# Two pairs of feed-forward input units by seven block products in place of eight, weight block sums on VectorE and by DMA

## The chip, the cores and the metric

The kernel runs on one core of a Trainium2 chip. The number that counts is the device time of one execution in microseconds (us). Three executions of the kernel before took 1249.81, 1249.92 and 1251.14 us; the median is 1249.92 us.

## What is computed

A decoder trunk of two layers on 256 tokens of width 1024, everything in float32. Each layer is a feed-forward half step, a mixer of three attention branches, and a second feed-forward half step, each followed by a residual sum and a layer norm. There are thus four feed-forward steps and two mixers. The change touches the feed-forward steps alone in what is computed:

```
D_MODEL = 1024;  SEQ = 256;  DEPTH = 2;  D_FF = 2816

def swiglu(x, w_in, w_out):
    gate, up = jnp.split(x @ w_in, 2, axis=-1)
    return (jax.nn.silu(gate) * up) @ w_out

for l in range(DEPTH):
    x = layer_norm(DN_ALPHA * x + 0.5 * swiglu(x, ffn1_in[l], ffn1_out[l]), ln_g[l, 0], ln_b[l, 0])
    x = layer_norm(DN_ALPHA * x + hybrid_mixer(x, ...), ln_g[l, 1], ln_b[l, 1])
    x = layer_norm(DN_ALPHA * x + 0.5 * swiglu(x, ffn2_in[l], ffn2_out[l]), ln_g[l, 2], ln_b[l, 2])
```

## The kernel before

**Tiles.** The tokens are two tiles of 128 (t = 0 and 1). The activations stand transposed in SBUF, eight blocks of 128 rows (the k of the code) by 128 tokens. Every float32 operand is split in two parts in the matmul's input format: a high part (`XH`, made by a copy on ScalarE) and a low part, the rest (`XL`, made by a subtraction on VectorE). One block product is three matmuls of 512 columns into a PSUM bank: high by high, high by low, low by high (lines 474, 475, 476, in `products`).

**Weights.** They come from HBM in chunks of 128 x 1024 float32, two blocks of k by 512 columns, on the SP queue (`weights`, line 230) into one of five buffers `raw`. ScalarE writes a chunk's high part (line 240) and VectorE its low part (line 249) into a pair of the 30 buffers `r`. A chunk is used by both token tiles, 2 x 2 x 3 = 12 matmuls, and its pair is then free again.

**A feed-forward step.** The 2816 hidden columns are 11 units of 256 columns. An input unit (`in_unit`) reads 256 gate and 256 up columns, side by side in one bank, over eight k: 4 chunks, and 8 x 3 = 24 matmuls for a token tile, 48 for both. Then `h_chain` makes silu(gate) times up (line 517 on ScalarE, line 519 on VectorE), transposes it on TensorE (line 371) and splits it (lines 383 and 385). An output unit (`out_unit`) multiplies it with its 256 rows of `w_out`: 2 chunks, 24 matmuls. The order is input unit u, then output unit u - 2.

**What sets the order.** The program is written once, in Python, by a planner. `items` is the list of chunk uses in order; the main loop at the end of the kernel steps a virtual clock `vt`, lets tile 1 follow tile 0 by up to `LAG` = 7 items, and between two block products issues whatever is due on the other engines, with estimated costs for VectorE (`V`), ScalarE (`A`) and the DMA. What it writes is fixed: on the chip each engine goes through its own list in that order and waits on semaphores.

**Layer norm.** `layer_norm` (lines 429 to 452) adds the output to the residual, takes mean and variance, subtracts and scales both halves of a tile's row (line 447, two instructions), then applies the reciprocal deviation and the bias to both halves (line 452, two instructions). After each half of line 452, `x_parts` transposes it for the next step. GpSimd computes the deviation's power (line 440) and issues the loads of gain and bias (`load_gb`, line 418).

## Time and profile before

| | before |
|---|---|
| median of three executions | 1249.92 us |
| the profiled execution | 1251.66 us, of which the trace's span is 1249.9 us |
| TensorE (PE) busy | 1236.2 us, 99% of the span |
| VectorE (DVE) busy | 883.8 us, 71% |
| ScalarE (ACT) busy | 640.9 us, 51% |
| DMA queues | 215.60 MB on the SP queue, 6.29 MB on GpSimd's |
| granted TensorE clock | 1.00 in every slice but the first (0.95) |

The span holds the six stages one after the other. By the matmuls' tiles the first feed-forward step runs to about 186 us, the first mixer to 431, the next two feed-forward steps to 623 and 811, the second mixer to 1048, the last feed-forward step to 1241; the rest is the last layer norm and the store. A busy TensorE in this profile is not a TensorE at its peak, since matmuls overlap: the distance from one matmul's start to the next one's tells what it costs.

### The profile page before, as it was taken

The page shows a single profiled execution, that of the slowest core. Times are in us where ns is not written, and L with a number is a line of the kernel's source. Part 1 is how long each engine was busy: PE and PEld are TensorE (multiplying, and loading weights), DVE is VectorE, ACT ScalarE, POOL GpSimd, SP SyncE. Part 2 cuts the span into 40 slices and gives each one's busy share as a digit, 9 for nine tenths or more (in the row PEclk, how much of TensorE's full clock was granted, in tenths as well). Part 3 has the DMA queues.
Part 4 walks back from the last instruction along what each step waited for, and adds up shares of the span by engine and source line. Part 5 has one row for each costly group of instructions (what it writes and reads, how often), then busy time and mean ns, then how long its engine had stood idle before and what let it go on. Part 6 is the DMA issues. An engine that isn't in the chain of part 4 may idle for free. (4 is left out here: it accounts for less than half of the span.)

```text
span 1249.9 us, 16651 instructions
## 1 busy us (share of the span) xinstructions
PE 1236.2 (99%) x5897; PEld 1025.5 (82%) x5897; DVE 883.8 (71%) x1533; ACT 640.9 (51%) x1005; POOL 32.5 (3%) x78
## 2 busy tenths in 40 slices
PE   8999999999999999999999999999999999999997
PEld 6888888888888888888888888888888887888886
DVE  6656559996999975555675555699979999655454
ACT  7544445566676554444444444454666756444340
POOL 0100000000000000000000000000000000000000
PEclk9999999999999999999999999999999999999999
DMA  9866656454535766655556655655444377656630
GB/s 313 267 183 197 203 150 183 132 150 144 179 102 178 237 207 203 204 181 176 172 186 227 203 182 179 170 152 156 146 136 153 101 222 237 216 170 200 185 118 34
DMA packets 173235, 222.95 MB, mean 178 GB/s; under 512 B 19040, under 2 KB 113248, under 8 KB 173152
## 3 DMA queue, kind: packets, MB, share of 16 engines
q1 hardware_dynamic: 171168, 215.60, 55.8%
q0 software_dynamic: 1984, 6.29, 1.6%
q8 instruction: 46, 0.75, 0.2%
q14 instruction: 37, 0.30, 0.1%
HBM read 220.80 MB, written 1.05 MB: 177 GB/s over the span
## 5 line engine op out<-in xcount | busy, mean ns | idle before, releaser
L249 DVE TENSOR_TENSOR r<-raw,r 128x1024 fp32r<-128x1024 f32 (+1 forms) x408 | 491.2, 1219 | 130.2 <-ACT r L240 77.8
L240 ACT ACTIVATE r<-raw 128x1024 fp32r<-128x1024 f32 (+1 forms) x408 | 420.0, 1052 | 125.5 <-PE bank L475 40.6
L474 PE MATMUL bank<-r,xh 128*128 128x512 f32 (+1 forms) x1184 | 468.9, 396 | 0.3 <-ACT xh L383 0.3
L476 PE MATMUL bank<-r,xl 128*128 128x512 f32 (+1 forms) x1184 | 461.9, 390 | 0.7 <-DVE xl L385 0.6
L475 PE MATMUL bank<-r,xh 128*128 128x512 f32 (+1 forms) x1184 | 461.3, 390 | 0.5 <-DVE r L249 0.5
L476 PEld LDWEIGHTS bank<-r,xl 128*128 128x128 f32 x1184 | 222.5, 188 | 48.4 <-DVE xl L385 2.0
L475 PEld LDWEIGHTS bank<-r,xh 128*128 128x128 f32 x1184 | 223.0, 188 | 43.1 <-DVE r L249 1.2
L474 PEld LDWEIGHTS bank<-r,xh 128*128 128x128 f32 x1184 | 222.8, 188 | 42.1 <-ACT xh L383 0.5
L474 PE MATMUL bank<-r,r 128*128 128x512 f32 x448 | 181.7, 406 | 0.0
L476 PE MATMUL bank<-r,r 128*128 128x512 f32 x448 | 175.7, 392 | 0.4 <-DVE r L385 0.4
L475 PE MATMUL bank<-r,r 128*128 128x512 f32 x448 | 175.1, 391 | 0.0
L517 ACT ACTIVATE f<-bank 128x256 f32<-128x256 f32 x88 | 33.8, 384 | 191.3 <-PE bank L476 190.4
L383 ACT ACTIVATE r<-bank 128x256 fp32r<-128x256 f32 (+1 forms) x120 | 52.2, 442 | 136.4 <-PE bank L371 136.2
L385 DVE TENSOR_TENSOR r<-bank,r 128x256 fp32r<-128x256 f32 (+1 forms) x120 | 58.3, 491 | 71.5 <-ACT r L383 71.3
L519 DVE TENSOR_TENSOR f<-f,bank 128x256 f32<-128x256 f32 x88 | 36.7, 417 | 96.0 <-ACT f L517 95.6
L476 PEld LDWEIGHTS bank<-r,r 128*128 128x128 f32 x448 | 84.1, 188 | 19.3 <-DVE r L385 1.2
L475 PEld LDWEIGHTS bank<-r,r 128*128 128x128 f32 x448 | 84.5, 189 | 14.7
L474 PEld LDWEIGHTS bank<-r,r 128*128 128x128 f32 x448 | 84.2, 188 | 14.2
L371 PE MATMUL bank<-ident,f 128*128 128x128 f32 x464 | 75.9, 273 | 0.6 <-DVE f L867 0.6
L371 PEld LDWEIGHTS bank<-ident,f 128*128 128x128 f32 x464 | 59.2, 141 | 20.5 <-DVE f L867 1.1
L791 ACT ACTIVATE f<-f,nb 128x128 f32<-128x128 f32 (+1 forms) x96 | 42.4, 445 | 9.0 <-DVE nb L783 8.7
L383 ACT ACTIVATE xh<-bank 128x512 fp32r<-128x512 f32 x32 | 18.6, 594 | 36.0 <-PE bank L371 36.0
(110 smaller groups left out, 691.8 us busy)
## 6 DMA issues: line engine op xcount, KB each, us to landing
raw<-in_ffn_in_dram SPq DMA_DIRECT2D x352, 256.0 KB, 3.7
raw<-in_w_in_dram SPq DMA_DIRECT2D x96, 512.0 KB, 3.6
raw<-in_ffn_out_dram SPq DMA_DIRECT2D x88, 512.0 KB, 4.9
raw<-in_w_out_dram SPq DMA_DIRECT2D x16, 512.0 KB, 4.7
raw<-in_w_br_a_dram SPq DMA_DIRECT2D x8, 512.0 KB, 4.2
raw<-in_w_br_c_dram SPq DMA_DIRECT2D x8, 512.0 KB, 4.1
raw<-in_w_br_b_dram SPq DMA_DIRECT2D x8, 512.0 KB, 3.7
f<-in_ln_g_dram POOLq DMA_DIRECT2D x12, 256.0 KB, 4.2
```

The costliest lines, as they stand in the source:

```text
L240: act.activation(pair[0].t[:, :n], raw_t[c % RAWS][:, :n], AF.Copy)
L249: dve.tensor_tensor(lo, raw_t[c % RAWS][:, :n], h.bitcast(F32), op=OP.subtract)
L371: pe.transpose(bank[:, j * 128:(j + 1) * 128], src[:, j * 128:(j + 1) * 128], ident)
L383: act.activation(hi, v, AF.Copy)
L385: dve.tensor_tensor(lo, v, hi.bitcast(F32), op=OP.subtract)
L474: pe.matmul(o, lhsT=xh(k), rhs=wh, start=k == 0, stop=False)
L475: pe.matmul(o, lhsT=xh(k), rhs=wl, start=False, stop=False)
L476: pe.matmul(o, lhsT=xl(k), rhs=wh, start=False, stop=k == nk - 1)
L517: act.activation(s.t[:, :256], ps.t[:, :256], AF.Silu)
L519: dve.tensor_tensor(s.t[:, 256:], s.t[:, :256], ps.t[:, 256:], op=OP.mult)
L791: act.activation(p.t[:, i * n:(i + 1) * n], p.t[:, i * n:(i + 1) * n], AF.Exp, bias=nb[:, h:h + 1], scale=SCALE, accum_out=den[:, h:h + 1])
```

## The change

The four input units 4, 5, 7 and 8 of a feed-forward step become two pairs, D4 (units 4 and 5) and D7 (7 and 8). A pair's work is a 2 x 2 block product: rows are the two token tiles, the inner dimension is the lower and the upper half of k (four k each), columns are 512 gate and 512 up columns. Eight block products of 12 matmuls are replaced by Strassen's seven (in Winograd's form), P1 to P7 (`double`). Each serves one chunk use, not two.

- The sums of activation blocks (`s_chain`): once in a feed-forward step, 10 additions or subtractions of 128 x 512 on VectorE and four splits, each a copy on ScalarE and a subtraction on VectorE.
- The sums of weight blocks: for a pair, two chunks of upper-half up weights are loaded into two double buffers `wide`; VectorE adds them to the gate chunks (line 328, 128 x 1024), later adds two more pairs of chunks. For P7 the lower-half up weights, already loaded once, are read again from HBM by a DMA on GpSimd's queue that adds to what stands in `wide` (line 318).
- The seven products need 14 prepared chunks (high and low part), where the two units needed 8.
- Results are put together in three PSUM banks: ScalarE copies a bank (line 707) before the next product accumulates onto it, VectorE adds or subtracts (lines 718 and 720). `c11`, `c21` and `h_pair` then make silu(gate) times up for 512 columns at once.
- The buffers: `raw` 5 to 7, `r` 30 to 28, small buffers `f` 16 to 12 and the two `wide` buffers, whose four halves also serve as `f`.
- Order: the string `FFN` gives the sequence of units. Near the pairs tile 1 follows by 2 items (`NEAR`). `layer_norm` now scales the second half (`centre(1)`) after the first half's line 452 work; the gain and bias load moves from unit 9 to unit 10.

```diff
-RAWS = 5
-NR = 30
+RAWS = 7
+NR = 28
+DEEP = 9
+EARLY = 2
 KEEP = 2
-NF = 16
+NF = 12
+FFN = "0 1 o0 2 o1 3 o2 D4 o3 6 o4 o5 D7 o6 9 o7 10 o8 o9 o10"
+NEAR = 2
...
+    wide_t = [tile_of(f"wide{i}", [128, 1024]) for i in range(2)]
+    f_t += [w[:, h * 512:(h + 1) * 512] for w in wide_t for h in range(2)]
...
     def weights(hold):
+        if sum_next[0] < len(sums):
+            n, pieces, c, chain, behind = sums[sum_next[0]]
+            ats = [low_at.get(b) for b in behind] if behind else [landed.get(chain)]
+            if None not in ats and max(ats) <= vt[0] + 1.0:
+                for view, ap in pieces:
+                    nc.gpsimd.dma_start(out=view(chain.view(n)), in_=ap, accum_op=OP.add)
+                clk["dma"] = max(clk["dma"], max(ats) + 0.5, vt[0] + 1.0) + 3.0
+                arrive[c] = clk["dma"] + 1.5
+                sum_next[0] += 1
+        if add_next[0] < len(adds):
+            c, other, there, behind, gone = adds[add_next[0]]
+            if (all(low_at.get(b, 1e9) <= vt[0] + AHEAD for b in behind)
+                    and max(arrive.get(there, 0.0), landed.get(there, 0.0)) <= vt[0] + AHEAD
+                    and (there in arrive or there in landed) and clk["dve"] <= vt[0] + AHEAD):
+                f = chunks[c].chain.view(1024)
+                dve.tensor_tensor(f, f, other(), op=OP.add)
+                low_at["sum", c] = V(1024)
+                arrive[c] = low_at["sum", c] + SEM
+                add_next[0] += 1
+                if gone is not None:
+                    give(gone, low_at["sum", c])
+        c = prep[high_next[0]] if high_next[0] < len(prep) else None
+        if (c in arrive and arrive[c] <= vt[0] + AHEAD and c - pos[0] < DEEP
                 and clk["act"] <= vt[0] + (1.0 if c - pos[0] < 3 else AHEAD)
-                and (pair := R.take_many(2, 0 if c - pos[0] < 3 else KEEP))):
-            n = chunks[c][0]
+                and (pair := R.take_many(2, 0 if c - pos[0] < 3 else KEEP + held[0]))):
...
+        def centre(h):
+            dve.scalar_tensor_tensor(y[:, hv[h]], y[:, hv[h]], mv[:, 0:1], (g0, g1)[h].t, op0=OP.subtract, op1=OP.mult)
             V(512)
+        centre(0)
+        if last:
+            centre(1)
         yield clk["dve"]
         for h, b in enumerate((b0, b1)):
-            hs = slice(h * 512, (h + 1) * 512)
+            hs = hv[h]
+            if h and not last:
+                centre(1)
...
+        def s_chain():
+            def tt(out, a, b, op):
+                dve.tensor_tensor(out, a, b, op=op)
+                return V(512) + 0.05
...
+            yield tt(a.t, h21, h22, OP.subtract)
+            yield tt(b.t, l21, l22, OP.subtract)
+            yield tt(a.t, a.t, b.t, OP.add)
+            yield from split("a2", a)
+            yield tt(b.t, a.t, h11, OP.subtract)
+            yield tt(b.t, b.t, l11, OP.subtract)
+            yield from split("s2", b)
+            yield tt(c.t, b.t, h12, OP.add)
+            yield tt(c.t, c.t, l12, OP.add)
+            yield from split("s4", c)
+            yield tt(a.t, h11, h21, OP.subtract)
+            yield tt(b.t, l11, l21, OP.subtract)
+            yield tt(a.t, a.t, b.t, OP.add)
+            yield from split("s3", a)
...
+            plan = (("P1", block_of(0, 0), X, True, None, lambda: copy("s1", X[0])),
+                    ("P5", sum_of("a2"), Yb, True, ("s", sub, "a2"), lambda: copy("s5", Yb[0])),
+                    ("P6", sum_of("s2"), X, False, ("s", sub, "s2"), lambda: copy("s2", X[0])),
+                    ("P3", sum_of("s4"), Yb, False, ("s", sub, "s4"), lambda: combine("s2", Yb[0], False, True)),
+                    ("P7", sum_of("s3"), X, False, ("s", sub, "s3"), lambda: combine("s5", X[0], True, False)),
+                    ("P2", block_of(0, 1), Z, True, None, c11),
+                    ("P4", block_of(1, 1), X, False, None, c21))
+            behind = {"P6": "s1", "P3": "s5", "P7": "s2", "P4": "s5+"}
+            chain = {"P1": cg, "P5": cg, "P6": cg, "P4": cg, "P7": cu}
...
+                    def body(t, ci=ci[name, c], c=c, hi=hi, lo=lo, bank=bank, first=first):
+                        o = bank[0].t
+                        for i in range(2):
+                            k = 2 * c + i
+                            wh, wl = (b.t[:, i * 512:(i + 1) * 512] for b in W[ci])
+                            pe.matmul(o, lhsT=hi(k), rhs=wh, start=first and k == 0, stop=False,
+                                      skip_group_check=not first)
+                            pe.matmul(o, lhsT=hi(k), rhs=wl, start=False, stop=False, skip_group_check=not first)
+                            pe.matmul(o, lhsT=lo(k), rhs=wh, start=False, stop=k == 3,
+                                      skip_group_check=not first)
+                            vt[0] += 3 * MM
+                            yield
...
+            for c in range(2):
+                loads.append((1024, G(top[c]), ci["P1", c], cg[c], False))
+            for c in range(2):
+                loads.append((1024, U(top[c]), None, cu[c], True))
+            for name, src, rows in (("P3", U, low), ("P2", G, low)):
+                for c in range(2):
+                    loads.append((1024, src(rows[c]), ci[name, c], None, False))
+            for c in range(2):
+                adds.append((ci["P5", c], lambda c=c: cu[c].view(1024), cu[c], (ci["P1", c],), None))
+            for c in range(2):
+                adds.append((ci["P6", c], lambda c=c: source(ci["P3", c]), ci["P3", c], (ci["P5", c], ci["P3", c]), ci["P3", c]))
+            for c in range(2):
+                adds.append((ci["P4", c], lambda c=c: source(ci["P2", c]), ci["P2", c], (ci["P6", c], ci["P2", c]), ci["P2", c]))
+            for c in range(2):
+                sums.append((1024, U(low[c]), ci["P7", c], cu[c], (("sum", ci["P5", c]),)))
+            for name in ("P1", "P5", "P3", "P6", "P2", "P7", "P4"):
+                prep.extend(ci[name, c] for c in range(2))
...
-        for u in range(NU):
-            in_unit(u)
-            if u > 1:
-                out_unit(u - 2)
-        out_unit(NU - 2)
-        out_unit(NU - 1)
+        steps = FFN.split()
+        doubles = [e for e in steps if e[0] == "D"]
+        if doubles:
+            hooks["x", sub, 1, 1] = s_chain
+        ramp = None
+        for e in steps:
+            n = len(items)
+            if e[0] == "D":
+                double(int(e[1:]), e == doubles[-1])
+                ramp = 0 if e == doubles[-1] else None
+            elif e[0] == "o":
+                out_unit(int(e[1:]))
+            else:
+                in_unit(int(e))
+            if doubles and e[0] != "D" and any(i.joint for i in items[-60:n]):
+                for it in items[n:]:
+                    if ramp is None:
+                        it.lag = NEAR
+                    else:
+                        ramp += 1
+                        it.lag = min(LAG, NEAR + ramp // 2)
...
-            for t in ((0, 1) if pos[0] - pos[1] < LAG else (1, 0)):
+            for t in ((0, 1) if pos[0] - pos[1] < (items[pos[0]].lag if pos[0] < N else LAG) else (1, 0)):
                 i = pos[t]
-                if i >= N or (t == 1 and i >= pos[0]) or i >= low_next[0] or low_at[i] + SEM > vt[0]:
+                if i >= N or (t == 1 and i >= pos[0]) or low_at.get(i, 1e9) + SEM > vt[0]:
                     continue
                 it = items[i]
-                if ready.get(it.need(t), 1e9) > vt[0]:
+                if it.joint and t:
+                    live = t, it, iter(())
+                    break
```

How the instructions move is shown at three places. The first two lie in the second feed-forward step of the first layer. TensorE before: tile 0 (`bank7_164`, with `xh0`, `xl0`) is at the first chunk of unit 5 and tile 1 (`bank2_159`) six items behind at the first chunk of unit 4, so that each chunk is used twice, in 12 matmuls.

```order
L474 MATMUL bank7_164<-r20_112,xh0_122 128x512
L475 MATMUL bank7_164<-r15_107,xh0_122 128x512
L476 MATMUL bank7_164<-r20_112,xl0_124 128x512
L474 MATMUL bank7_164<-r20_112,xh0_122 128x512
L475 MATMUL bank7_164<-r15_107,xh0_122 128x512
L476 MATMUL bank7_164<-r20_112,xl0_124 128x512
L474 MATMUL bank2_159<-r13_105,xh1_123 128x512
L475 MATMUL bank2_159<-r26_118,xh1_123 128x512
L476 MATMUL bank2_159<-r13_105,xl1_125 128x512
L474 MATMUL bank2_159<-r13_105,xh1_123 128x512
L475 MATMUL bank2_159<-r26_118,xh1_123 128x512
L476 MATMUL bank2_159<-r13_105,xl1_125 128x512
```

TensorE after, in the pair D4 of the same step: the second chunk of P2 (`bank7_162`, tile 0's upper-k blocks) and the first chunk of P4 (`bank3_158`, tile 1's). A row's first `r` is the weight chunk's high or low part.

```order
L784 MATMUL bank7_162<-r27_119,xh0_120 128x512
L786 MATMUL bank7_162<-r4_96,xh0_120 128x512
L787 MATMUL bank7_162<-r27_119,xl0_122 128x512
L784 MATMUL bank7_162<-r27_119,xh0_120 128x512
L786 MATMUL bank7_162<-r4_96,xh0_120 128x512
L787 MATMUL bank7_162<-r27_119,xl0_122 128x512
L784 MATMUL bank3_158<-r13_105,xh1_121 128x512
L786 MATMUL bank3_158<-r16_108,xh1_121 128x512
L787 MATMUL bank3_158<-r13_105,xl1_123 128x512
L784 MATMUL bank3_158<-r13_105,xh1_121 128x512
L786 MATMUL bank3_158<-r16_108,xh1_121 128x512
L787 MATMUL bank3_158<-r13_105,xl1_123 128x512
```

A chunk now serves six matmuls and the next six need another pair of `r`; P4 accumulates onto the bank that P7 wrote 12 matmuls earlier. VectorE before, from output unit 1 to input unit 4: a subtraction for each chunk (L249), with the units' small work (L519, L385) between them.

```order
L249 TENSOR_TENSOR r5_97<-raw1_127,r1_93 128x1024
L385 TENSOR_TENSOR r4_96<-bank6_163,r4_96 128x256
L249 TENSOR_TENSOR r25_117<-raw2_128,r12_104 128x1024
L249 TENSOR_TENSOR r26_118<-raw3_129,r13_105 128x1024
L519 TENSOR_TENSOR f13_145<-f13_145,bank0_157 128x256
L249 TENSOR_TENSOR r17_109<-raw4_130,r6_98 128x1024
L385 TENSOR_TENSOR r7_99<-bank1_158,r7_99 128x256
L249 TENSOR_TENSOR r28_120<-raw0_126,r22_114 128x1024
L249 TENSOR_TENSOR r16_108<-raw1_127,r11_103 128x1024
L519 TENSOR_TENSOR f5_137<-f5_137,bank7_164 128x256
```

VectorE after, in D4: L348 is the chunk's subtraction (L249 before), L328 the sum of two weight chunks, L720 the sum of a copied bank and a bank. `wide0` and `wide1` here have been added to by GpSimd's DMA.

```order
L328 TENSOR_TENSOR raw4_128<-raw4_128,raw3_127 128x1024
L630 TENSOR_TENSOR f5_137<-f5_137,bank7_162 128x256
L348 TENSOR_TENSOR r4_96<-raw5_129,r27_119 128x1024
L328 TENSOR_TENSOR raw1_125<-raw1_125,raw5_129 128x1024
L348 TENSOR_TENSOR r14_106<-wide0_144,r25_117 128x1024
L490 TENSOR_TENSOR r26_118<-bank6_161,r26_118 128x256
L348 TENSOR_TENSOR r5_97<-wide1_145,r19_111 128x1024
L348 TENSOR_TENSOR r16_108<-raw4_128,r13_105 128x1024
L720 TENSOR_TENSOR f6_138<-bank5_160,f6_138 128x512
L348 TENSOR_TENSOR r20_112<-raw1_125,r11_103 128x1024
L720 TENSOR_TENSOR f1_133<-f1_133,bank3_158 128x512
L348 TENSOR_TENSOR r22_114<-raw6_130,r0_92 128x1024
```

Sums of chunks and of banks now stand between the subtractions; the second L720, which reads P7's bank and stands behind the subtraction for P4's second chunk, is what P4 on TensorE waits for. The sums of `wide0` and `wide1` for P5, after which GpSimd's DMA may write to them, stand 20 and 18 rows ahead of the two subtractions that read them here.

The third place is VectorE at the end of the second mixer, where tile 0's layer norm meets the last split for tile 1 (`xl1`). Before:

```order
L438 TENSOR_SCALAR rs0_71<-mv0_69 128x1
L249 TENSOR_TENSOR r6_98<-raw2_128,r25_117 128x1024
L447 SCALAR_TENSOR_TENSOR y0_131<-y0_131,mv0_69,f10_142 128x512
L447 SCALAR_TENSOR_TENSOR y0_131<-y0_131,mv0_69,f11_143 128x512
L385 TENSOR_TENSOR xl1_125<-bank6_163,xh1_123 128x512
L452 SCALAR_TENSOR_TENSOR y0_131<-y0_131,rs0_71,f15_147 128x512
L452 SCALAR_TENSOR_TENSOR y0_131<-y0_131,rs0_71,f4_136 128x512
L249 TENSOR_TENSOR r26_118<-raw3_129,r12_104 128x1024
```

After, the same place (L553 is line 447 before, L563 line 452, L490 line 385):

```order
L543 TENSOR_SCALAR rs0_71<-mv0_69 128x1
L348 TENSOR_TENSOR r16_108<-raw6_130,r15_107 128x1024
L553 SCALAR_TENSOR_TENSOR y0_131<-y0_131,mv0_69,f11_143 128x512
L490 TENSOR_TENSOR xl1_123<-bank6_161,xh1_121 128x512
L563 SCALAR_TENSOR_TENSOR y0_131<-y0_131,rs0_71,f7_139 128x512
L553 SCALAR_TENSOR_TENSOR y0_131<-y0_131,mv0_69,f6_138 128x512
L563 SCALAR_TENSOR_TENSOR y0_131<-y0_131,rs0_71,wide0_144 128x512
L348 TENSOR_TENSOR r26_118<-raw0_124,r20_112 128x1024
```

One instruction on tile 0's second half now stands behind the split for tile 1 and behind the first half's last step.

## Rows read from the trace of the kernel before

**Rows 1.** Page, part 1: engine, busy us, share of the span, instructions.

```profile
PE 1236.2 (99%) x5897; PEld 1025.5 (82%) x5897; DVE 883.8 (71%) x1533; ACT 640.9 (51%) x1005; POOL 32.5 (3%) x78
```

**Rows 2.** Lines by form: line, engine, form, count, busy us, mean ns, idle before.

```profile
L475 PE MATMUL bank<-r,xh 128*128 128x512 f32 x1152 | 449.6, 390 | 0.5 <-DVE r L249 0.5
...
L249 DVE TENSOR_TENSOR r<-raw,r 128x1024 fp32r<-128x1024 f32 x400 | 482.4, 1221 | 129.9 <-ACT r L240 77.8 <-issue 24.8 <-PE bank L476 16.3
...
L240 ACT ACTIVATE r<-raw 128x1024 fp32r<-128x1024 f32 x400 | 412.3, 1054 | 115.8 <-PE bank L475 35.6 <-PE bank L476 19.3 <-DMA raw<-in_w_out_dram 16.1
...
L385 DVE TENSOR_TENSOR r<-bank,r 128x256 fp32r<-128x256 f32 x88 | 37.1, 422 | 69.6 <-ACT r L383 69.6
L519 DVE TENSOR_TENSOR f<-f,bank 128x256 f32<-128x256 f32 x88 | 36.7, 417 | 96.0 <-ACT f L517 95.6
...
L385 DVE TENSOR_TENSOR r<-bank,r 128x512 fp32r<-128x512 f32 x32 | 21.2, 683 | 1.8 <-ACT r L383 1.7
...
L1011 ACT ACTIVATE f<-bank 128x512 f32<-128x512 f32 x24 | 14.3, 597 | 8.4 <-PE bank L476 8.0
...
L597 DVE TENSOR_TENSOR f<-f,f 128x512 f32<-128x512 f32 x20 | 13.8, 692 | 0.7
```

**Rows 3.** Windows by stage: first mixer, second feed-forward step (busy us, counts).

```profile
186.00:431.00 245.00, 244.51 (x1259) 206.47 (x1259) 222.47 (x489) 149.81 (x271) 6.59 (x7) 1.00 0.54 164
431.00:623.00 192.00, 191.57 (x876) 157.63 (x875) 113.72 (x140) 87.53 (x118) 5.33 (x7) 1.00 0.60 189
```

**Rows 4.** Windows by slice, the same columns: one feed-forward, three mixer slices.

```profile
500.00:531.00 31.00, 31.00 (x142) 25.54 (x142) 17.39 (x20) 14.03 (x18) 0.00 (x0) 1.00 0.65 204
...
218.75:250.00 31.25, 31.25 (x158) 26.66 (x157) 30.04 (x70) 17.27 (x25) 0.00 (x0) 1.00 0.44 132
...
343.75:375.00 31.25, 31.25 (x171) 26.61 (x170) 30.01 (x82) 22.17 (x53) 0.00 (x0) 1.00 0.35 102
375.00:406.25 31.25, 30.94 (x157) 25.45 (x157) 30.43 (x76) 21.35 (x42) 2.22 (x4) 1.00 0.54 179
```

**Rows 5.** Timeline, TensorE, 21 matmuls in a feed-forward step: start, length, instruction.

```profile
126.30 0.39 PE L474 MATMUL bank<-r,xh 128*128 128x512 f32 x1
...
130.83 0.39 PE L476 MATMUL bank<-r,xl 128*128 128x512 f32 x1
```

**Rows 6.** Timeline, VectorE and TensorE, around 622: chunks' subtractions, transposes.

```profile
621.41 2.35 DVE L249 TENSOR_TENSOR r<-raw,r 128x1024 fp32r<-128x1024 f32 x2
...
622.33 1.03 PE L371 MATMUL bank<-ident,y 128*128 128x128 f32 x8
```

**Rows 7.** Timeline, VectorE, second mixer's last layer norm, tile 0.

```profile
1047.47 1.41 DVE L447 SCALAR_TENSOR_TENSOR y<-y,mv,f 128x512 f32<-128x512 f32 x2
1048.79 0.68 DVE L385 TENSOR_TENSOR xl<-bank,xh 128x512 fp32r<-128x512 f32 x1
1049.39 1.41 DVE L452 SCALAR_TENSOR_TENSOR y<-y,rs,f 128x512 f32<-128x512 f32 x2
```

**Rows 8.** Timeline, TensorE, at the same place.

```profile
1048.59 0.39 PE L474 MATMUL bank<-r,xh 128*128 128x512 f32 x1
1048.82 0.39 PE L475 MATMUL bank<-r,xh 128*128 128x512 f32 x1
1049.53 0.49 PE L476 MATMUL bank<-r,xl 128*128 128x512 f32 x1 [0.32 <-DVE xl L385]
1050.19 0.66 PE L371 MATMUL bank<-ident,y 128*128 128x128 f32 x4 [0.17 <-DVE y L452]
```

**Rows 9.** DMA issues: tensors, queue, count, KB each, median us to landing.

```profile
raw<-in_ffn_in_dram SPq DMA_DIRECT2D x352, 256.0 KB, 3.7
...
raw<-in_ffn_out_dram SPq DMA_DIRECT2D x88, 512.0 KB, 4.9
...
f<-in_ln_g_dram POOLq DMA_DIRECT2D x12, 256.0 KB, 4.2
```

**Rows 10.** Timeline, VectorE and GpSimd at 388: a DMA's issue beside a subtraction.

```profile
387.86 1.22 DVE L249 TENSOR_TENSOR r<-raw,r 128x1024 fp32r<-128x1024 f32 x1
388.07 0.58 POOL L418 DMA_DIRECT2D f<-in_ln_g_dram  x1 [185.05 <-DVE f L867]
```

More of the change, by code (lines that the diff above doesn't have):

```diff
@@ L104, in take_many, with __init__, take, free @@
         return [self.take() for _ in range(n)]
+class Pairs:
+    def __init__(self, pool, tiles):
+        self.pool, self.tiles = pool, tiles
+        self.first = len(pool.tiles) - 2 * len(tiles)
+    def take(self):
+        for i, t in enumerate(self.tiles):
+            own = [e for e in self.pool.tiles if e[1] - self.first in (2 * i, 2 * i + 1) and e[0] <= self.pool.now[0]]
+            if len(own) == 2:
+                for e in own:
+                    self.pool.tiles.remove(e)
+                return Pair(self, i, t, own)
+        return None
+class Pair:
+    def __init__(self, pool, i, t, own):
+        self.pool, self.i, self.t, self.own = pool, i, t, own
+    def free(self, at):
+        self.pool.pool.tiles += [(at,) + e[1:] for e in self.own]
 class Halves:
@@ new lines, with __init__, view @@
+    RAW = Free(raw_t, vt)
+    WIDE = Pairs(F, wide_t)
+    raw_of = {}
+    held = [0]
+    class Chain:
+        def __init__(self):
+            self.buf = None
+        def view(self, n):
+            return self.buf.t[:, :n]
+    class Chunk:
+        def __init__(self, n, chain=None, last=False):
+            self.n, self.chain, self.last = n, chain, last
+    def add_chunk(width, pieces):
+        chunks.append(Chunk(width))
+        c = len(chunks) - 1
+        loads.append((width, pieces, c, None, False))
+        prep.append(c)
+        return c
@@ L248, in weights @@
             h, lo = (b.t[:, :n] for b in W[c])
-            dve.tensor_tensor(lo, raw_t[c % RAWS][:, :n], h.bitcast(F32), op=OP.subtract)
+            dve.tensor_tensor(lo, source(c), h.bitcast(F32), op=OP.subtract)
             low_at[c] = V(n)
             low_next[0] += 1
+            if (c in raw_of and not chunks[c].last) or (chunks[c].chain and chunks[c].last):
+                give(c, low_at[c])
     pool.memset(ident, 0.0)
@@ L1147 @@
         if next(g, 0) == 0:
-            if it.done:
+            if it.done and not (it.joint and t):
                 it.done(t)
-            if t == 1:
-                for b in W.pop(pos[1]):
+            if t == (0 if it.joint else 1):
+                for b in W.pop(pos[t]):
                     b.free(vt[0])
```

186 lines of the change are left out of this document (156 added, 30 removed).

## The prediction

> **What bounds the kernel now.** I read the page's busy shares first. TensorE is busy 99% of the span, VectorE 71%, ScalarE 51% [rows 1]. Since a busy TensorE need not be a fast one, the timeline comes next. In a feed-forward step 21 matmuls of 512 columns start between 126.30 and 130.83, so 20 steps take 4.53 us, 0.2265 us each [rows 5]; a matmul's own length of 0.39 us overlaps the next two. The lines by form then tell who holds TensorE up: in 1152 matmuls of line 475 it idled 0.5 us, all for the chunks' low parts [rows 2]. TensorE's list, matmul behind matmul, is thus the time, and a matmul taken out gives 0.2265 us as long as the other engines still deliver.
>
> Whether they would is read by stage. In the second feed-forward step VectorE is busy 113.7 of 192 us and ScalarE 87.5 [rows 3], in a slice inside it 17.4 and 14.0 of 31 us [rows 4]. In the mixer VectorE is busy 222.5 of 245 us, in its fullest slices 30.0 of 31.25, and TensorE still lost nothing in two of the three slices shown and 0.31 us in the third [rows 4]. So this kernel runs VectorE at 96% beside a full TensorE, where the work lies well spread.
>
> **TensorE: what goes.** A pair of units took 2 x 48 matmuls; seven products of 12 take 84. With two pairs in each of four steps, 8 x 12 = 96 matmuls go: 96 x 0.2265 = 21.7 us. The transposes keep their number (eight for a pair). The order shows the same form, 512 columns with a 128-column stationary block, so the price of those left should stay. Bounds: 21.7 if nothing waits, below that by the waits further down.
>
> **VectorE: what comes.** By step, with durations of rows 2: 12 more chunk subtractions (1.221 us) 14.7; 12 sums of chunks 128 x 1024, not in the trace, between 1.22 (the subtraction of that size) and 1.38 (twice the 512-column addition of 0.692), taken at 1.22 since the size is the same, 14.7; `s_chain` 10 x 0.692 + 4 x 0.683 = 9.7; six bank sums 4.2; four products and four splits at 512 columns for eight of each at 256: 4 x (0.692 + 0.683) - 8 x (0.417 + 0.422) = -1.2. Together +42 us, 113.7 to 156 of some 186 us: 84%. That average hides the dense part. From D4's first matmul to D7's last (D4 o3 6 o4 o5 D7) TensorE has 2 x (84 x 0.2265 + 1.0) + 3 x 24 x 0.2265 + 48 x 0.2265 + 0.5 = 67.8 us, the transposes at 1.03 us for eight [rows 6]. VectorE has for a pair 20 x 1.221 + 3 x 0.692 + 2 x 0.69 + 2 x 0.683 = 29.2, for the output units 6 x 1.221, for unit 6 4 x 1.221 + 4 x 0.42: 72.4 us in all. But records overlap: two subtractions in a row take 2.35 us, so the second adds 1.13 [rows 6]; by that step the work is 72.4 x 1.13 / 1.22 = 67 us. VectorE is at 99 to 107% of TensorE there. In front of it, in the 62 us of four input and three output units, it is at the 56% of rows 4 plus `s_chain`'s 9.7 us, 72%, and can run ahead.
>
> What TensorE loses by it: at least nothing, since two of the mixer's fullest slices lost nothing; at most 4 x (72.4 - 67.8) = 18 us, if VectorE enters each dense part without any chunk ahead. The nearest row is the mixer slice with 0.31 us lost. I take that for each pair: 8 x 0.31 = 2.5 us.
>
> The adds inside a pair are new waits too. P4 must not start until VectorE has summed P7's bank. In the order P2's 12 matmuls stand between, 2.72 us. The chain needs the last matmul's 0.39, the sum's 0.69 and one subtraction in front of it (the order has P4's own second chunk there), 1.22: 2.30 us. It fits with 0.4 to spare; what queues behind that sum on VectorE is the next units' chunks. P6 and P7 wait for a copy by ScalarE (0.60 us, perhaps behind a chunk's copy of 1.05) and have 12 matmuls as cover as well.
>
> **ScalarE and the DMA.** ScalarE gets 12 x 1.054 + 10 x 0.597 us more for a step and some for the wider silu, about 20: 87.5 to 108 of 186, nothing on the path. The queues get 1 MB more for a pair, 2.1 on 36 MB in a step (192 us at 189 GB/s), at a DMA share of 0.60 [rows 3]: nothing by itself.
>
> The accumulating DMA is not in the trace. Its cover can be counted in VectorE's list: between the sum that frees `wide1` and the subtraction that reads it stand 13 instructions of 1024 columns and four of 256: 13 x 1.13 + 4 x 0.42 = 16.4 us, less ScalarE's copy of 1.05: 15.3. Plain transfers land in 4.2 us (256 KB, GpSimd's queue) and 4.9 (512 KB, SP's) [rows 9]. Twice the longer, 10 us, for a read and a write of the destination, would still be covered. I take nothing for it; its bounds are 0 and the rival below. That GpSimd can issue at all beside a full VectorE is seen at 388, where its DMA took 0.58 us inside a subtraction of 1.22 that reads two SBUF operands [rows 10]. The Trainium skill (SBUF — State Buffer, "Who interferes with whom") says that GpSimd is locked out, and with it the descriptors of its DMAs, while VectorE runs a copy or tensor-scalar in its two-port mode, but that a tensor-tensor has no such mode. By the first half, stretched to all of VectorE's work, the cover would be used up and the rival below would come; by the second half the sum stands. The row at 388 agrees with the second half.
>
> **Layer norm and mixers.** At the end of the second mixer a matmul starts 0.71 us after its forerunner, and the transposes 0.66 after that [rows 8]: 0.48 and 0.43 us over the pitch, waiting for `xl` and then `y` on VectorE, which stand behind two instructions of line 447, 1.41 us [rows 7]. The change takes one of them, 0.66 us, out from in front of both. What is late next is the same chain, shorter. Two mixer ends give at most 1.8 us, at least 0; I take 1.0. Against that the mixers run with 28 `r` buffers for 30: between 0 and 16 slices x 0.31 = 5 us, taken at 0.6, since TensorE waits there for hardly anything now.
>
> **Sum.** The profiled execution took 1251.66 us, 1.76 of it outside the span. 1251.66 - 21.7 + 2.5 - 1.0 + 0.6 = 1232.1. It lay 1.74 us above the median of the runs, 1249.92, so the forecast for the median is 1230.3.
>
> **Rivals.**
> First, VectorE sets the pace in the pairs. For it: 99 to 107% in the dense part, and six matmuls, 1.36 us, now use up a chunk that costs VectorE 1.13 to 1.22 and often a sum of 1.22 besides. In the first step of all it also makes the rotary tables and masks. Against it: the mixer rows, and more than a quarter of its time idle ahead of the pairs. Price: up to the 18 us in place of 2.5, that is 1246; with two subtractions ahead of P7's sum another 8 x 0.8. The likely part is 1235 to 1247.
> Second, and on the other side: the accumulating DMA lands later than its cover of 15.3 us. Then ScalarE's copy of `wide` waits at the head of its list, every chunk behind it waits too, and TensorE stands for the excess in each of 8 pairs. It decides from 15.3 + 22.1 / 8 = 18.1 us on, where the whole gain and 0.2% are gone; at 20 us it costs 8 x 4.7 = 38 and the time is 1268. For it: nothing in the trace adds to memory by DMA. Against it: 18 us is over four times the 4.2.
> Third, the change might not do what it says, TensorE's list being no shorter. The order excludes it: each chunk of a pair serves six matmuls and there are 14 chunks. What stays possible is a gain above the forecast, with no wait in the pairs and all 1.8 us at the mixer ends: 1226.
>
> **Chances.** The forecast (1226 to 1235) 0.68; VectorE sets the pace 0.20, of which 0.03 ends within 0.2% of before (1247.4 to 1252.4, about what a measurement of this kernel can tell from no change); the late DMA 0.08; below 1226 0.04. That gives faster 0.89, same 0.03, slower 0.08. The range, 1225 to 1239, holds the forecast, most of what lies below, and the nearer third of the first rival: about 8 in 10.
>
> **What would show it.** Right: TensorE's matmul records fall by 96, the pitch stays at 0.2265, VectorE's busy time rises by about 168 us to 1050, and TensorE idles under half a microsecond in a pair. The chunk sums read 1.2 us, the DMA on GpSimd's queue lands within 10. Wrong: gaps on TensorE in P3, P7 or P4 with the low parts (L348) or the bank sums as releaser speak for the first rival; ScalarE idle before its copy of `wide`, released by that DMA, for the second. If the pitch itself is longer in the pairs, the first term was mis-sized.

## The result and the profile after

The changed kernel takes 1229.8 us, the kernel before on the same chip 1250.87: a ratio of 0.9831 (95% interval [0.9817, 0.9844], so too below), 21.1 us less. Of its six executions five took 1229.19 to 1230.32 us; the sixth took 1312.55 us at a granted clock of 0.876, where the others had 0.997 or 0.998, and stands in the median (1229.48 without it) but not in the ratio. The forecast was 1230.3. The profiled execution took 1229.19 us with a span of 1227.4, so that span against span 22.5 us went.

The page's first part, in the order of [rows 1]:

```profile
PE 1213.3 (99%) x5801; PEld 1007.1 (82%) x5801; DVE 1028.8 (84%) x1677; ACT 697.3 (57%) x1061; POOL 50.5 (4%) x94
```

TensorE has 96 instructions fewer and is as full as before. VectorE has 144 more and its busy time rose by 145 us. Where the gain lies is seen by stage: first mixer, second feed-forward step, and in it the stretch from the first matmul of D4 to the last of D7 (columns as in [rows 3]: the stretch and its length; busy us and count of TensorE, its weight loads, VectorE, ScalarE and GpSimd; granted clock; DMA share and GB/s):

```profile
181.00:426.00 245.00, 243.61 (x1254) 205.15 (x1253) 223.24 (x489) 147.81 (x271) 6.72 (x7) 1.00 0.53 162
426.00:611.00 185.00, 185.00 (x846) 152.87 (x846) 148.18 (x174) 103.31 (x133) 9.18 (x10) 1.00 0.67 208
488.40:563.30 74.90, 74.90 (x339) 61.97 (x338) 64.19 (x65) 48.40 (x59) 4.63 (x6) 1.00 0.72 219
```

The stretch of the feed-forward step went from 192 to 185 us and TensorE is busy in all of it, with VectorE at 80%. The mixer, which the change hardly touches, lost 0.9 us of TensorE's time that it did not lose before (243.61 for 244.51).

What the new operations cost, by line and form (columns as in [rows 2]): the sums of chunks (L328), GpSimd's issue of the accumulating DMA (L318), the matmuls on a chunk's low part in the four products of a pair that use sums of activations (L786), the sums of a product's bank (L720).

```profile
L786 PE MATMUL bank<-r,r 128*128 128x512 f32 x128 | 49.9, 390 | 0.3 <-DVE r L348 0.3
...
L328 DVE TENSOR_TENSOR raw<-raw,raw 128x1024 f32<-128x1024 f32 x32 | 39.0, 1218 | 0.0
...
L328 DVE TENSOR_TENSOR raw<-raw,wide 128x1024 f32<-128x1024 f32 x16 | 19.5, 1222 | 2.9 <-DMA wide<-in_ffn_in_dram 2.6
L318 POOL DMA_DIRECT2D wide<-in_ffn_in_dram x16 | 19.5, 1216 | 319.4 <-DVE raw L328 233.2 <-DVE f L425 46.7 <-PE bank L587 36.8
...
L720 DVE TENSOR_TENSOR f<-bank,f 128x512 f32<-128x512 f32 x8 | 5.5, 690 | 8.8 <-PE bank L787 8.8
```

A sum of 1024 columns takes 1.22 us as estimated. In 128 matmuls of L786 TensorE idled 0.3 us, once, and no other line of the pairs shows a wait: the pairs cost it next to nothing. The transfers, answering to [rows 9] (last number: median us to landing):

```profile
wide<-in_ffn_in_dram SPq DMA_DIRECT2D x16, 512.0 KB, 6.2
wide<-in_ffn_in_dram POOLq DMA_DIRECT2D x16, 512.0 KB, 7.2
...
f<-in_ln_g_dram POOLq DMA_DIRECT2D x12, 256.0 KB, 6.4
```

The accumulating DMA lands 7.2 us after its issue (6.1 to 10.9 over the 16). What it is covered by is seen on the tile `wide` in one pair of the third step (view: operations on one tile; duration min, median, max; first and last start):

```profile
L328 DVE TENSOR_TENSOR raw<-raw,wide x2: 1224/1226/1227, 655.4 to 665.6; 128x1024 f32<-128x1024 f32 x2
L318 POOL DMA_DIRECT2D wide<-in_ffn_in_dram x2: 1217/1237/1257, 657.3 to 667.4; - x2
L340 ACT ACTIVATE r<-wide x2: 1050/1051/1052, 679.9 to 681.5; 128x1024 fp32r<-128x1024 f32 x2
```

The second sum ends at 665.6 + 1.2 = 666.8, its DMA is issued at 667.4, and ScalarE copies the result at 681.5: 14.7 us of cover, of which issue and landing use about 0.6 + 7.2. This is the shortest cover of the 16 (the longest is 23.3 us); the landing closest to its reader left 5.7 us.

**Where the 22.5 us of span come from.** I listed every gap between the starts of two matmuls over the pitch of 0.228 us in both traces. 96 matmuls of that pitch are 21.9. At the stage borders 3.4 us of gaps went (before: 0.46 at 194, 0.86 at 432, 0.75 at 623, 0.46 at 811, 0.91 at 1049; after: none). In the mixers gaps grew by 3.5 (0.36 us in each before; now 2.14 and 2.08). In the pairs one gap is new, 0.6 with the short step behind it, at 84.60. 21.9 + 3.4 - 3.5 - 0.6 = 21.2; of the other 1.3 us 0.7 lies in the first 14 us, where gaps and the lower clock cost 4.6 for 5.3 before, and the rest probably in gaps too short for the list. That start costs 3.8 to 5.6 in the profiled executions of the other runs, so its 0.7 is no effect of the change.

At a border the new order of the layer norm reads so, VectorE first, then TensorE:

```profile
425.14 0.74 DVE L553 SCALAR_TENSOR_TENSOR y<-y,mv,f 128x512 f32<-128x512 f32 x1
425.81 0.68 DVE L490 TENSOR_TENSOR xl<-bank,xh 128x512 fp32r<-128x512 f32 x1
426.41 0.74 DVE L563 SCALAR_TENSOR_TENSOR y<-y,rs,f 128x512 f32<-128x512 f32 x1
427.07 0.74 DVE L553 SCALAR_TENSOR_TENSOR y<-y,mv,f 128x512 f32<-128x512 f32 x1
```

```profile
428.09 0.39 PE L587 MATMUL bank<-r,xl 128*128 128x512 f32 x1
428.32 0.60 PE L476 MATMUL bank<-ident,y 128*128 128x128 f32 x4
```

One L553 stands ahead of `xl` where two stood in [rows 7], and the transposes follow their forerunner by 0.23 us where [rows 8] had 0.66. That the new order does this here is not shown: `e3_ln_old` below has the old order and no gap at this place either. The costliest gap that the change brought is in the mixer at 382.76, TensorE first:

```profile
382.76 0.39 PE L587 MATMUL bank<-r,xl 128*128 128x512 f32 x1
384.07 0.70 PE L476 MATMUL bank<-ident,f 128*128 128x128 f32 x4 [0.91 <-DVE f L1176]
```

```profile
380.33 2.35 DVE L348 TENSOR_TENSOR r<-raw,r 128x1024 fp32r<-128x1024 f32 x2
382.60 0.68 DVE L1232 TENSOR_TENSOR r<-wide,r 128x512 fp32r<-128x512 f32 x1
...
383.66 0.61 DVE L1176 TENSOR_SCALAR f<-f,den 128x256 f32<-128x256 f32 x2
```

TensorE wants the attention's output `f`; its last operation (L1176) stands behind two chunk subtractions that were issued ahead of it.

### The profile page after: what moved, and what is told of

Its sections match the earlier page's. It is cut to its first block, busy times and chain, and to the rows that moved or that the text cites. A ratio compares the mean times of both kernels' runs of the same rounds, so it can differ in the third digit from the quotient of the medians.

```text
span 1227.4 us, 16445 instructions
## 1 busy us (share of the span) xinstructions
PE 1213.3 (99%) x5801; PEld 1007.1 (82%) x5801; DVE 1028.8 (84%) x1677; ACT 697.3 (57%) x1061; POOL 50.5 (4%) x94
## 4 chain that ended last, share of the span: by engine, by line
PE 91%; DVE 7%; ACT 1%; issue 1%; DVEq 0%; ACTq 0%
PE bank L586 24%; PE bank L587 23%; PE bank L585 23%; PE bank L476 5%; PE bank L786 4%; PE bank L787 4%; PE bank L784 4%; DVE r L348 2%; PE bank L1024 1%; PE bank L1023 1%; PE bank L1196 1%; PE bank L1129 1%; DVE r L974 0%; DVE iacc L1054 0%; ACT r L340 0%
## 5 line engine op out<-in xcount | busy, mean ns | idle before, releaser
L348 DVE TENSOR_TENSOR r<-raw,r 128x1024 fp32r<-128x1024 f32 (+1 forms) x440 | 526.4, 1217 | 49.8 <-ACT r L340 35.6
L340 ACT ACTIVATE r<-raw 128x1024 fp32r<-128x1024 f32 (+1 forms) x440 | 449.1, 1052 | 78.3 <-PE bank L587 17.6
L585 PE MATMUL bank<-r,xh 128*128 128x512 f32 (+1 forms) x928 | 369.5, 398 | 0.0
L586 PE MATMUL bank<-r,xh 128*128 128x512 f32 (+1 forms) x928 | 361.8, 390 | 1.1 <-DVE r L348 1.1
L587 PE MATMUL bank<-r,xl 128*128 128x512 f32 (+1 forms) x928 | 361.9, 390 | 0.0
L587 PEld LDWEIGHTS bank<-r,xl 128*128 128x128 f32 x928 | 174.2, 188 | 36.7 <-DVE xl L490 0.2
L586 PEld LDWEIGHTS bank<-r,xh 128*128 128x128 f32 x928 | 174.7, 188 | 34.9 <-DVE r L348 2.8
L585 PEld LDWEIGHTS bank<-r,xh 128*128 128x128 f32 x928 | 174.5, 188 | 31.9 <-ACT r L340 0.2
L585 PE MATMUL bank<-r,r 128*128 128x512 f32 x448 | 179.8, 401 | 0.0
L587 PE MATMUL bank<-r,r 128*128 128x512 f32 x448 | 175.1, 391 | 0.0
L586 PE MATMUL bank<-r,r 128*128 128x512 f32 x448 | 174.9, 390 | 0.1
L628 ACT ACTIVATE f<-bank 128x256 f32<-128x256 f32 x54 | 20.7, 382 | 114.2 <-PE bank L587 113.8
L490 DVE TENSOR_TENSOR r<-bank,r 128x256 fp32r<-128x256 f32 (+1 forms) x104 | 55.6, 542 | 29.8 <-ACT r L488 28.8
L476 PE MATMUL bank<-ident,f 128*128 128x128 f32 x388 | 61.6, 273 | 2.3 <-DVE f L1176 2.3
L476 PEld LDWEIGHTS bank<-ident,f 128*128 128x128 f32 x388 | 48.6, 140 | 18.0 <-DVE f L1176 4.3
L786 PE MATMUL bank<-r,r 128*128 128x512 f32 x128 | 49.9, 390 | 0.3 <-DVE r L348 0.3
L784 PE MATMUL bank<-r,r 128*128 128x512 f32 x128 | 49.9, 390 | 0.0
```

The costliest lines, as they stand in the source:

```text
L340: act.activation(pair[0].t[:, :n], source(c), AF.Copy)
L348: dve.tensor_tensor(lo, source(c), h.bitcast(F32), op=OP.subtract)
L476: pe.transpose(bank[:, j * 128:(j + 1) * 128], src[:, j * 128:(j + 1) * 128], ident)
L490: dve.tensor_tensor(lo, v, hi.bitcast(F32), op=OP.subtract)
L585: pe.matmul(o, lhsT=xh(k), rhs=wh, start=k == 0, stop=False)
L586: pe.matmul(o, lhsT=xh(k), rhs=wl, start=False, stop=False)
```

## The experiments

Each was timed beside the kernel before on the same chip; "gap" is a start-to-start time over the pitch.

**No pairs, all else as changed** (`e1_no_pairs`).

```
-FFN = "0 1 o0 2 o1 3 o2 D4 o3 6 o4 o5 D7 o6 9 o7 10 o8 o9 o10"
+FFN = "0 1 2 o0 3 o1 4 o2 5 o3 6 o4 7 o5 8 o6 9 o7 10 o8 o9 o10"
```

> The changed kernel with all its buffers, the new layer norm order and the new planner, but with the units one by one (no pairs, no sums, no accumulating DMA). Theory A (the gain is the 96 matmuls at 0.228 us; the stalls won at the stage borders, 3.4 us, and lost in the mixers, 3.5 us, come from the rest of the change): 1250 us, 1249 to 1252, with TensorE gaps at the borders gone and those in the mixers still there. Theory B (part of the gain comes from the rest, or the pairs' matmuls cost more than their pitch and hide a gain): 1246 or less.

Measured: 1251.46 us, ratio 1.0004 [0.9995, 1.0014]. The border gaps are gone and the mixers' new gaps are there (0.48 at 270.95, 1.09 at 388.5). So the other edits about cancel, and the pairs alone are worth 1251.46 - 1229.8 = 21.7 us, against 21.9 for 96 matmuls less 0.6 for their one gap.

**The layer norm's order alone, in the kernel before** (`e2_ln_only`).

```
+        centre(0)
+        if last:
+            centre(1)
...
+            if h and not last:
+                centre(1)
```

> The kernel before with the layer norm's new order alone. Theory A (that order takes away the TensorE gaps at the five stage borders): 1247.0 us, 1246 to 1248.5, with the gaps of 0.86 us at 432 and 0.91 us at 1049 gone. Theory B (the gaps went because tile 1 or the weights stand elsewhere in the new order): 1250 us and the gaps stay.

Measured: 1248.44 us, ratio 0.9982 [0.9973, 0.9991]: 2.4 us. At the mixers' ends the gap of 0.91 is gone, and of the 0.86 at 432 about 0.4 is left. **The same taken out of the changed kernel** (`e3_ln_old`: `centre(0)` and `centre(1)` both up front).

> The changed kernel with the layer norm's old order (both halves of the subtraction first). Theory A (the order alone gave the 2.6 us that it gave by itself): 1232.4, 1231.5 to 1233.5, with gaps at the borders again. Theory B (in the changed kernel the borders are covered by something else, too): 1229.5 to 1230.5.

Measured: 1231.6 us, ratio 0.9845 [0.983, 0.9859]: 1.8 us more than the changed kernel, though the two intervals overlap a little. Its trace shows what came back, after the second feed-forward step (TensorE):

```profile
613.27 1.03 PE L476 MATMUL bank<-ident,y 128*128 128x128 f32 x8
614.55 0.50 PE L582 MATMUL bank<-r,xh 128*128 128x512 f32 x1 [0.25 <-ACT xh L488]
```

The gaps are at the ends of feed-forward steps (190, 614, 796), not at those of the mixers, on which my term had rested. At the first mixer's end the transposes follow without a gap, with the old order:

```profile
429.73 0.39 PE L584 MATMUL bank<-r,xl 128*128 128x512 f32 x1
429.97 0.60 PE L476 MATMUL bank<-ident,y 128*128 128x128 f32 x4
```

The second mixer's end reads the same (1036.33, 1036.57). So another part of the change closes the mixers' ends, 1.8 of the 3.4 us that went at the borders, without the new order too; which part is open. The layer norm's order gives 2.4 us in the kernel before and 1.8 in the changed one.

**The buffers back to 5 raw and 30 `r`** (`e4_bufs`).

```
-RAWS = 7
-NR = 28
+RAWS = 5
+NR = 30
```

> The changed kernel with 5 raw and 30 r buffers, as before, in place of 7 and 28. Theory A (the mixers lose 3.5 us because 28 r buffers shorten the lead of the weights): mixers' gaps fall from 4.2 us to about 0.7, the pairs lose up to 2 us for want of raw buffers; 1226 to 1228. Theory B (the mixers lose by another order of VectorE's list, whatever the buffers): mixers' gaps stay near 4 us; 1229 to 1232.

Measured: 1228.23 us, ratio 0.9816 [0.98, 0.9833]. The mixers' gaps fall back to 0.36 us each; the gap shown above at 382.76 is now

```profile
382.69 1.25 PE L476 MATMUL bank<-ident,f 128*128 128x128 f32 x8
384.25 0.63 PE L476 MATMUL bank<-ident,f 128*128 128x128 f32 x4 [0.31 <-DVE f L1176]
```

The buffers are thus the cause of the mixers' loss; whether the 7 `raw` or the 28 `r` are, no run separates. Two chunk subtractions stand ahead of L1176 here too (from 378.58 on). What differs is TensorE's list: it comes to the transposes 4.1 us after those subtractions start, in the changed kernel 2.7 us after (380.33 to 382.99). Of the 3.5 us only 0.9 came back in the span (1226.5) and 1.6 in the median, since the first feed-forward step now lost 1.7 (0.76 at 144.8, 0.92 at 155.46) and the start 1.1 (which, as said, differs from execution to execution).

**Three pairs for two, the first from unit 2 on** (`e5_three`).

```
+FFN = "0 1 o0 D2 o1 4 o2 o3 D5 o4 7 o5 o6 D8 o7 10 o8 o9 o10"
```

> The changed kernel with three pairs in a step in place of two (D2, D5, D8): 48 matmuls fewer, 10.9 us, and some 16 us more of VectorE in each step, 164 of about 175 us. Theory A (VectorE keeps up as long as it stays under about 96% over a step): 1219 to 1224. Theory B (VectorE sets the pace in dense stretches, and two pairs were the limit): the gaps on TensorE in the pairs grow to over 8 us and the time is 1228 or more.

Measured: 1248.9 us, ratio 0.9984 [0.9974, 0.9993]. 48 more matmuls are gone (10.9 us), and yet the gain is lost: the gaps add up to 37.0 us, for 9.3 in the changed kernel. What TensorE waited for (view of waits: total us, times, longest):

```profile
PE bank L787 <- DVE r L665: 10.4, 5, 3.3
PE bank L784 <- ACT r L663: 4.7, 4, 2.3
```

Both lines are the splits of the activations' own sums, not weight chunks: D2 starts before VectorE has got through the ten sums of `s_chain`, which every pair of the step needs. VectorE's list there (482.67 is the split for which TensorE waited) holds them between the pair's chunks:

```profile
479.20 0.69 DVE L654 TENSOR_TENSOR f<-f,f 128x512 f32<-128x512 f32 x1
479.80 0.68 DVE L720 TENSOR_TENSOR f<-bank,f 128x512 f32<-128x512 f32 x1
480.40 2.35 DVE L348 TENSOR_TENSOR r<-raw,r 128x1024 fp32r<-128x1024 f32 x2
482.67 0.69 DVE L665 TENSOR_TENSOR r<-f,r 128x512 fp32r<-128x512 f32 x1
```

The time is what the rival that VectorE has no more room gave, the place is not. The next run tells them apart.

**Three pairs, all later** (`e10_three_late`): the same number of matmuls and of VectorE operations.

```
+FFN = "0 1 o0 2 o1 D3 o2 5 o3 o4 D6 o5 o6 D8 o7 10 o8 o9 o10"
```

> Three pairs again, but later in the step (D3, D6, D8 for D2, D5, D8), with one more input unit in front of the first. Theory A (the first three-pair order lost its gain because the activation sums, L663 and L665, were not ready when the first pair's P5 to P7 came, and because TensorE's clock fell to half in those gaps; not for want of VectorE's throughput): the long gaps and the half-clock stretches go, 1219 to 1228. Theory B (VectorE's throughput is the limit with three pairs): gaps move to L348 and the bank sums, 1235 or more.

Measured: 1226.29 us, ratio 0.9798 [0.9783, 0.9814]. In the second to fourth step the long gaps are gone (0.3 us is left in each); the first, where VectorE also makes tables and masks, still lost 6.3 us for 0.6 in the changed kernel, part of it to chunks that were late (L348). No wait for L663 or L665 is left. So in `e5_three` it was the lead before the first pair, not VectorE's sum over the step.

**VectorE loaded on purpose** (`e9_dve`): each summed chunk's subtraction done twice, 48 x 1.13 = 54 us more.

```
+            for _ in range(2 if ("sum", c) in low_at else 1):
```

> The changed kernel with the subtraction of each summed chunk done twice (six more of 128 x 1024 for each pair, 48 in all, at 1.13 us: 54 us of VectorE), which the planner does not know of. Theory A (VectorE has idle time in the pairs, 10 to 11 us of 75 in the dense part by the changed kernel's trace, and up to 15 us of chunks ahead): some 2 us late in each pair, 1240 to 1255. Theory B (VectorE sets the pace in the pairs already): all of it shows, 1275 to 1284.

Measured: 1241.76 us, ratio 0.9924 [0.9906, 0.9943]: 54 us of work cost 12.0 of time. The dense stretch of the second step and TensorE's waits:

```profile
488.00:566.00 78.00, 77.39 (x350) 63.63 (x349) 75.73 (x77) 49.49 (x62) 5.90 (x8) 1.00 0.71 216
```

```profile
PE bank L785 <- DVE f L721: 4.9, 7, 1.5
PE bank L787 <- DVE r L349: 2.8, 5, 0.9
```

At 97% VectorE is late: in this step TensorE loses 0.75 us in each pair, where P4 waits for the sum of P7's bank (L721). In the first step, where VectorE has the tables and masks besides, the gaps are 6.7 us for 0.6. The changed kernel, at 86% in the same place, has room, and not much.

**The accumulating DMA delayed** by memsets of 128 x 104 on GpSimd ahead of its issue: 15 (`e7_delay_short`) and 50 (`e8_delay_long`). A memset of one column on VectorE, into the same tile (`fill` in the trace), lets them start.

```
+                dve.memset(slow[:, :1], 0.0)
+                for _ in range(15):
+                    pool.memset(slow, 0.0)
```

> The changed kernel with 15 memsets of 128 x 104 on GpSimd, about 3 us by the 0.2 us that one of 128 x 128 took, in front of each accumulating DMA and behind a one-column memset on VectorE that it waits for. In the changed kernel's trace 14 to 20 us lie between that DMA's issue and ScalarE's first read, and it lands in 7.2. Theory A (the DMA is hidden with 7 us to spare): no change, 1229 to 1231. Theory B (a late landing is already paid for somewhere): 8 x 2 x 2 us or more, 1250 and up.

Measured: 1229.68 us, ratio 0.9826 [0.9803, 0.9849]: hidden altogether. The DMA goes out 3.7 to 6.7 us after the sum for 0.3 to 0.6 in the changed kernel, and the landing closest to its reader leaves 1.1 us.

> The same with 50 memsets, about 9.5 us for each DMA and, since the two of a pair are issued 2.5 to 6 us apart on one queue, 13 to 17 us for the second. Theory A (the cover is the 14 to 20 us that stand between issue and read): each pair now waits for about 6 us, ScalarE idles before its copy of wide, released by that DMA, and the time is 1265 to 1290. Theory B (the order leaves far more room than that): under 1240.

Measured: 1312.66 us, ratio 1.0489 [1.0462, 1.0516], 83 us above the changed kernel, more than expected. GpSimd in the first pair of the second step:

```profile
504.43 12.04 POOL L319 MEMSET fill<- 128x104 f32 x50 [37.38 <-DVE fill L317]
516.90 1.26 POOL L321 DMA_DIRECT2D wide<-in_ffn_in_dram  x1 [0.42 <-issue]
517.68 12.54 POOL L319 MEMSET fill<- 128x104 f32 x50
530.58 1.22 POOL L321 DMA_DIRECT2D wide<-in_ffn_in_dram  x1 [0.36 <-issue]
```

A pair has two such DMAs, and their delays stand one behind the other: the second went out 23 us after the sum that freed `wide` (506.3 + 1.2), where 13 to 17 had been expected. ScalarE then waited for the landing of the second:

```profile
ACT r L343 <- DMA wide<-in_ffn_in_dram: 56.5, 8, 9.5
```

But the run also stops VectorE, which it was not meant to do. The one-column memset for the second DMA writes the tile that GpSimd's first 50 memsets are still writing, and VectorE's list stands until they end:

```profile
506.29 1.22 DVE L331 TENSOR_TENSOR raw<-raw,wide 128x1024 f32<-128x1024 f32 x1
516.52 1.22 DVE L351 TENSOR_TENSOR r<-raw,r 128x1024 fp32r<-128x1024 f32 x1 [9.01 <-issue]
```

Each of the eight pairs has such a stop; it ends 0.04 us after the last of those memsets, and the eight add up to 66 us. TensorE waits behind both:

```profile
PE bank L787 <- ACT f L710: 30.8, 7, 6.7
PE bank L479 <- DVE f L633: 22.7, 4, 6.6
```

The first line is ScalarE's copy of a bank, which stands behind its wait for the landing. The second is the product of silu(gate) and up, each of the four times 0.8 to 3.1 us after one of VectorE's stops. The clock takes part too: after the wait of 6.7 us at 540 the matmuls' pitch is 0.427 us, the 1.2 GHz level, until 545, and 60 such steps in the run lose 12 us. So a landing behind its cover is paid for by ScalarE and TensorE, as my second rival says, but its price is not shown: the 83 us hold VectorE's stops as well. The cover holds the delays of the short run, and not the 18 to 24 us of the second DMAs here.

**Two pairs in the first step and three late ones in the others.** 36 matmuls fewer than in the changed kernel, 8.2 us; the three runs differ in the buffers.

```
+FFN3 = "0 1 o0 2 o1 D3 o2 5 o3 o4 D6 o5 o6 D8 o7 10 o8 o9 o10"
...
+        steps = (FFN if sub == 0 else FFN3).split()
```

With 5 raw and 30 `r` (`e13_mixed_bufs`):

> Two pairs in the first step (beside the rotary tables), three late pairs in the other three steps, and 5 raw and 30 r buffers. Theory A (the three effects add: 36 matmuls fewer than in the changed kernel, 8.2 us, and the mixers' 3.5 us back, less the waits of 1.7 us that 5 raw buffers cost in the first step): 1219 to 1222. Theory B (three pairs need the seven raw buffers, so that the pairs lose what the mixers gain): 1224 or more.

Measured: 1237.09 us, ratio 0.9881 [0.9865, 0.9898]. What `e4_bufs` gained in the mixers does not carry over: gaps of 24.7 us in all, in pairs and at their ends, some with the lower clock behind them. With 6 and 29 (`e14_mixed_29`):

> The same pairs with 6 raw and 29 r buffers. Theory A (the mixers' loss is a matter of the r buffers, one by one): mixers' gaps between 0.7 and 4.2 us, 1220 to 1223. Theory B (the loss comes from one place in the mixer where the order tips over): gaps as with 28 or as with 30.

Measured: 1225.79 us, ratio 0.9797 [0.9782, 0.9811]; over half of the mixers' loss is gone, and new gaps stand in the pairs (1.2 at 489 and at 1092) and at a border (1.5 at 790). With 7 and 28, as in the changed kernel (`e15_mixed_28`):

> Two pairs in the first step, three late pairs in the other three, with the changed kernel's 7 raw and 28 r buffers. Theory A (three late pairs cost nothing outside the first step, where they met the rotary tables and masks on VectorE and lost about 6.6 us): 1226.3 - 6.6 + 12 x 0.228 = 1222.4, 1221 to 1224. Theory B (the first step's loss moves to the next places as soon as the order shifts): 1225 or more.

Measured: 1223.64 us (1222.59 to 1224.92), ratio 0.9779 [0.9765, 0.9792]: the fastest, 6.2 us under the changed kernel. Its second feed-forward step (the stretch holds some 3 us of the next one) and its waits:

```profile
426.00:611.00 185.00, 185.00 (x848) 152.63 (x847) 166.01 (x189) 110.16 (x140) 12.16 (x13) 1.00 0.69 216
```

```profile
PE bank L787 <- DVE r L349: 0.3, 1, 0.3
```

VectorE stands at 90% over a whole step, and TensorE's waits in all pairs are this one of 0.3 us. Of the 8.2 us the span (1221.8) shows 5.6: the start lost 0.9, and the rest went into some ten gaps of 0.1 in the pairs and the end.

## Why the prediction was right

**The main term held.** 96 x 0.2265 = 21.7 was forecast; the traces give 21.9, and `e1_no_pairs` 21.7 for the pairs alone. The pitch did not change.

**VectorE's work was counted rightly, its share in the dense part was not.** The +168 us came from record lengths; their sum (count by mean over all of VectorE's groups) rose from 951.8 to 1118.2, by 166. Busy time rose by 145 only, since overlapping records count once there. The step that failed is the 99 to 107% for D4 to D7. I gave TensorE 67.8 us for that stretch, by the units in the order's text; it took 74.9, because 36 more matmuls of the units before and after stand inside it (156 of lines 585 to 587 where I counted 120; 36 x 0.2265 = 8.2) and six transposes fewer. VectorE was busy 64.2 us there, not 67 to 72, and so at 86%. The waits in the pairs were 0.6 us for my 2.5.

**The P4 chain held, with more to spare than counted**: no gap at P4 in the changed kernel. In D4 of the second step the sum of P7's bank reads so on VectorE, and P4's first matmul so on TensorE:

```profile
508.54 1.21 DVE L348 TENSOR_TENSOR r<-raw,r 128x1024 fp32r<-128x1024 f32 x1
510.58 0.69 DVE L720 TENSOR_TENSOR f<-f,bank 128x512 f32<-128x512 f32 x1 [0.83 <-PE bank L787]
```

```profile
513.10 0.39 PE L784 MATMUL bank<-r,xh 128*128 128x512 f32 x1
```

The subtraction that I had put into the chain was over 0.8 us before P7's last matmul was, and the sum waited for the bank alone. It ended 1.8 us before P4, and 1.0 us or more before it in all eight pairs, for my 0.4. In `e9_dve`, where that subtraction stands there twice, P4 is 0.6 to 1.7 us late.

**The accumulating DMA** landed in 7.2 us in the median for "within 10" (one of 16 took 10.9), its shortest cover was 14.7 for 15.3, and no time was lost. GpSimd's issues were not held up beside a full VectorE: they took 1.19 to 1.26 us, and the three that had no VectorE instruction beside them 1.26 too. The Trainium skill (SBUF — State Buffer, "Who interferes with whom") says that a tensor-tensor has no two-port mode and that in a probe it did not stall a DMA as a copy did. The trace agrees, with issues 0.3 to 0.6 us after the end of the sum that releases them.

**Layer norm: -1.0 forecast, -1.8 to -2.4 measured** (3.4 us of gaps in the traces). The mechanism is real in the kernel before, where the order alone takes 1.4 of 1.8 us at the mixers' ends. The place was wrong for the changed kernel: there the mixers' ends, which I had priced, have no gap without it either, and it gives 1.8 at the ends of the feed-forward steps, which I had put at nothing (`e3_ln_old`).

**Mixers with 28 `r`: +0.6 forecast, +3.5 measured**, inside the bound of 5. I took the lower end because TensorE hardly waited there. `e4_bufs` shows the buffers to be the cause, `raw` and `r` changed together. The costliest wait there is for the attention's output, by the place of its transposes in TensorE's list, and not for a chunk without its `r`; VectorE's busy time in the first mixer is as before (223.2 for 222.5).

**The sum is better than its parts.** In the profiled execution I forecast 1251.66 - 19.6 = 1232.1 and it took 1229.19: 2.9 too high. Pairs 1.9 and layer norm 2.4 too dear, mixers 2.9 too cheap, and 1.3 that no step had. The 1.74 us taken off for the median hid most of the difference: this time the profiled execution lay 0.6 below the median and not above it. That the forecast comes within 0.5 us of the measured median is luck; what was right is the term of 21.7 and that no other term is above 4 us.

**The rivals.** The first does not hold at two pairs, nor at three placed late outside the first step; `e9_dve` shows where it begins. The second needs the DMA over 6 us later than it was issued here, and its price is open. The third was excluded by the counts.

## What to carry to other kernels

On this saturated TensorE a matmul saved by a block product paid its full pitch, once the helper engines' one-time sums were done before the first such block: the place of the blocks was worth 23 us (`e5_three` against `e10_three_late`), with the same work. Judge a helper engine over the stretch as it is issued, with what the order interleaves, and load it on purpose once: 54 us of extra work for 12 of time tells what room is left. Look at what else a delay put in for a test holds up: in `e8_delay_long` it stopped VectorE too. Price new numbers of buffers in the stages that don't need them; in the mixers they cost 3.5 us, and giving it back cost more where more pairs were wanted (`e13_mixed_bufs`).
